# Two loads behind each product for the sample operands, and a step's exponentials written behind the split of the step before

## The chip, the cores and the metric

The kernel runs as one program on one core of a Trainium2 chip. The core has five engines that run side by side and wait for each other through semaphores: TensorE (PE, matrix products, with PEld for its weight loads), VectorE (DVE), ScalarE (ACT), GpSimd (POOL) and SyncE (SP, which here only issues transfers). The metric is the device time of one execution in microseconds (us), lower is better, as the median of several runs.

## The reference

One layer of a decoder is computed for a prompt of 1024 positions and for 8 samples of 8 positions each (64 more columns), with width 1024, all in fp32:

```python
def layer(x, ...):
    h = rmsnorm(x, norm_mix)
    q, k, v, gu, gv, ga, gb = split_in(h @ w_in)
    o  = sink_attention over a window of 128 keys      # 16 heads, 4 kv heads, blocks of 128 queries
    vn = layernorm(gelu(gv));  s = gelu(gu) * (tril(W_s) @ vn + b)   # 128-position chunks, 6 groups
    merged = sigmoid(ga) * (o @ w_branch_attn) + sigmoid(gb) * (s @ w_branch_gmlp)
    x = x + merged @ w_out
    x = x + conv_ffn(rmsnorm(x, norm_ffn))             # up, depthwise conv of width 3, gelu gate, down

def sink_attention(q, k, v, mask, sinks):
    s = where(mask, q @ k.T / 8, -1e30);  m = max(s.max(-1), sink)
    p = exp(s - m);  return (p / (p.sum(-1) + exp(sink - m))) @ v
```

The samples attend to 128 cached keys and values and to their own 8. The last keys and values, the convolution's state and the normalised v rows are outputs too. Both groups end in a final RMSNorm.

## The kernel before

**Operands.** An fp32 product is made of three fp32r products: each operand is split into a high part (a cast on ACT, line 40) and a low part (a subtraction on DVE, line 41), and PE multiplies high by high, high by low and low by high. `split(hi, lo, src)` is this pair. The large products are done by a scheme with seven products of half size (`Chain.product`, line 297).

**Weights.** The class `Weights` keeps the stream of weight tiles: `load` issues the transfers into `wraw` on SP (line 147), `emit` splits a tile into `wh` and `wl`, `get` returns the next one and runs ahead by a given number.

**The columns** are two groups: group 0 has the 64 sample columns and 512 prompt columns, group 1 the other 512.

**The stage of the projections** goes through a list `seq` of column tiles, with seven products each, and calls `behind(at, j)` after each product j. `behind` takes one finished job from `done` (`a_finish`: an activation on ACT, and a store of a gate tile `z` to `sg0d` or `sg1d` on SP, line 874), and then one of three kinds of side work: `jobs`, `lns`, or, when these are used up, `prep`. For the last two entries of `seq`, `prep` holds what `prepare_samples` returns, twelve jobs that only issue transfers and some copies: the queries, keys and masks of the samples, `load_s(0, ...)` for the six operands `s` of group 0 of the gating branch (line 881, 576 KB each), and the caches `ckt` and `cvc` of the samples (line 912). They go out one behind each product with j from 1 to 6.

**The attention stage** runs `attention(gr, pieces)` once for each group. `pieces` are parts of other products (line 237, the gating branch under group 0, the first merge under group 1), nine or twelve matmuls each; `fill()` puts some of them between the attention's steps so that PE has work while a softmax is under way. Under group 0 the samples' attention comes first (`sc_s`, `tr_s`, `pv_s`, `out_s`: scores, transposes, product with v, output); its exponentials are at line 1140. Then the prompt's 16 steps (4 kv heads by 4 blocks) go through a software pipeline, one turn of which, for turn i, is written as:

- `tr_p` of step i-2: four transposes on PE into the one `pt` bank (line 1249), the split of `pt` into `ph` on ACT and `pl` on DVE, and a product `c` on POOL;
- `fill()`;
- `sc_p` of step i: eight score matmuls into `sc` (line 1220), a copy to `s` on ACT (line 1228), a masked copy on DVE (1230, or 1233 for the first block), the row maximum `nm` on DVE (1236), four exponentials with row sums on ACT (1239), reciprocal and multiplication on DVE (1241, 1242);
- `fill()`;
- `pv_p` of step i-3: products with v into `po` (1272, 1277, 1280), a copy `ot` on ACT (1283), two additions `of` on DVE (1288), and the split of `of` into `oh` and `ol`.

**The order.** Each engine does its instructions in one fixed order. This order is made when the program is built, by a scheduler that starts from the written order as a priority and takes an instruction that it holds ready. So a change of the written order can move instructions of every engine in the neighbourhood. Each transfer uses one of eight semaphores in turn, and waits on SP until the transfer eight before it has landed; SP issues in order, so a store that waits for its data holds back the loads behind it.

Of the kernel before, what the change touches and what calls it, by code (L numbers as in the profile page):

```python
# [34 lines left out]
def layer(tc, a):  # L35
# [11 lines left out]
    with ExitStack() as top:  # L47
# [307 lines left out]
        with ExitStack() as ph1:  # L355
# [609 lines left out]
            done, prep, qko = [], [], ExitStack()  # L965
            late["qk"] = poola("qk", 1, qko)

            def behind(at, j):

                if done:  # L970
                    done.pop(0)()
                if jobs:
                    jobs.pop(0)()
                elif lns and at > 5 and j in (0, 2, 4, 6):
                    lns.pop(0)()
                elif prep and j:
                    prep.pop(0)()

            for at, (pair, gs, whole) in enumerate(seq):
                if at == 6:  # L980
# [19 lines left out]
                if gs[0] == 0:  # L1000
# [5 lines left out]
                    prep = prepare_samples()  # L1006
# [88 lines left out]
            def attention(gr, pieces):  # L1095
# [8 lines left out]
                def fill():  # L1104
                    slots["at"] += 1
                    if prep:
                        prep.pop(0)()
                    left = slots["of"] - slots["at"]
                    want = slots["at"] * slots["n"] // (slots["of"] + 4) if left >= 5 else (
                        slots["n"] - (slots["n"] - slots["done"]) * left // (left + 1))  # L1110
                    while slots["done"] < want:
                        pieces[slots["done"]]()
                        slots["done"] += 1
# [3 lines left out]
                if has_s:  # L1117
                    st = {}
# [84 lines left out]
                with tc.tile_pool(name=f"at{g}", bufs=1) as ap:  # L1203
                    gap(ap, (256, 128)[g])
                    steps = [(kv, i) for kv in range(NKV) for i in range(nblk)]
                    st = {}

                    def sc_p(kv, i):
                        if i == 0 and not has_s:
                            oh[kv], ol[kv] = (act.tile([P, 2, n], F32R, name=f"o{x}{kv}") for x in "hl")  # L1210
                        b = gr["blk0"] + i
                        cur = P * i + (P if g else 0)
                        k0 = cur - P if b else cur
                        o0 = 0 if b else P
                        ps = psm.tile([P, 1024], F32, name="sc")
                        ps = ps.rearrange("p (h j) -> p h j", h=4)
                        for h in range(4):
                            q = qt[2 * kv + h // 2][:, h % 2, soff + P * i:soff + P * i + P]
                            for e in range(2):
                                PE.matmul(ps[:, h, o0:256], q, kst[kv][:, e, k0:cur + P],  # L1220
                                          start=e == 0, stop=e == 1)
                        if i == 0:
                            gr["operands"](kv + 1)()
                        if i == 3:
                            gr["values"](kv + 1)()
                        s = ap.tile([P, 4, 132], F32, name="s", bufs=3)[:, :, 0:P + 1]
                        G.tensor_copy(s[:, :, P], late["sinkb"][:, 4 * kv:4 * kv + 4])
                        S.copy(s[:, :, 0:P], ps[:, :, P:256])
                        if b:
                            V.copy_predicated(s[:, :, 0:P], late["mprev"].to_broadcast([P, 4, P]),  # L1230
                                              ps[:, :, 0:P])
                        else:
                            V.copy_predicated(s[:, :, 0:P], late["mprev"].to_broadcast([P, 4, P]),
                                              late["neg"][:, :, None].to_broadcast([P, 4, P]))
                        nm = ap.tile([P, 4], F32, name="nm", bufs=3)
                        V.tensor_reduce(nm, s, AX.X, ALU.max, negate=True)
                        dn = ap.tile([P, 4], F32, name="dn", bufs=3)
                        for h in range(4):
                            S.activation(s[:, h], s[:, h], AF.Exp, bias=nm[:, h:h + 1],  # L1239
                                         accum_out=dn[:, h:h + 1])  # L1240
                        V.reciprocal(dn, dn)
                        V.tensor_mul(s[:, :, 0:P], s[:, :, 0:P], dn[:, :, None].to_broadcast([P, 4, P]))  # L1242
                        st[kv, i] = s

                    def tr_p(kv, i):
                        s = st.pop((kv, i))
                        pt = pst.tile([P, 512], F32, name="pt")
                        for h in range(4):
                            PE.transpose(pt[:, h * P:h * P + P], s[:, h, 0:P], ident)  # L1249
                        ph = ap.tile([P, 512], F32R, name="ph", bufs=2)  # L1250
                        pl = ap.tile([P, 512], F32R, name="pl", bufs=2)
                        split(ph, pl, pt)
                        parts = []
                        if gr["blk0"] + i:
                            c = ap.tile([P, 512], F32R, name="c", bufs=2)
                            cs, fs, ls = (x.rearrange("p (h e q) -> p h e q", h=4, e=2) for x in (c, ph, pl))
                            for src, swap in ((fs, 0), (ls, 1)):
                                for e in range(2):
                                    r, w = 64 * e, 64 * (e ^ swap)
                                    G.affine_select(cs[w:w + 64, :, e], src[r:r + 64, :, e].bitcast(F32),  # L1260
                                                    [[0, 4], [1 - 2 * e, 64]], ALU.is_ge, 0.0, base=-e,
                                                    channel_multiplier=2 * e - 1)
                            parts = [cs]
                        st[kv, i] = [ph, pl, *parts]

                    def pv_p(kv, i):
                        ph, pl, *c = st.pop((kv, i))
                        po = pst.tile([P, 512], F32, name="po")
                        v, d, b = gr["vst"][kv], gr["dvst"][kv], gr["blk0"] + i - gr["b0"]
                        if not c:  # L1270
                            for e, x in enumerate((ph, pl)):
                                PE.matmul(po, v[:, 0], x, start=e == 0, stop=e == 1)
                        else:
                            half = lambda x, e: x.rearrange("p (h e q) -> p h e q", h=4, e=2)[:, :, e]
                            for e in range(2):
                                for x in (ph, pl):
                                    PE.matmul(half(po, e), v[:, b - 1 + e], half(x, e),  # L1277
                                              start=e == 0 and x is ph, stop=False, skip_group_check=True)
                            for e in range(2):
                                PE.matmul(half(po, e), d[:, e, b - 1], c[0][:, :, e], start=False, stop=True,  # L1280
                                          skip_group_check=True)
                        t = ap.tile([64, 512], F32, name="ot")
                        S.copy(t, po[64:128])
                        of = ap.tile([P, 2, P], F32, name="of", bufs=2)
                        tv = t.rearrange("p (a r q) -> p a r q", a=2, r=2)
                        pv = po[0:64].rearrange("p (a r q) -> p a r q", a=2, r=2)
                        for par in range(2):
                            V.tensor_add(of[64 * par:64 * par + 64], pv[:, :, par], tv[:, :, par])
                        c0 = soff + P * i
                        split(oh[kv][:, :, c0:c0 + P], ol[kv][:, :, c0:c0 + P], of)  # L1290

                    for i in range(len(steps) + 3):
                        if i == len(steps):
                            os_.append([(oh[kv][:, e], ol[kv][:, e]) for kv in range(NKV) for e in range(2)])
                        if 2 <= i < len(steps) + 2:
                            tr_p(*steps[i - 2])
                        fill()
                        if i < len(steps):
                            sc_p(*steps[i])
                        if i < len(steps) + 2:  # L1300
                            fill()
                        if i >= 3:
                            pv_p(*steps[i - 3])
# [657 lines left out]
```

## Time and profile before

| | |
|---|---|
| median of 3 runs | 1519.22 us (1518.84 to 1520.51) |
| the profiled execution, its own time | 1514.99 us |
| its span, first to last instruction | 1513.2 us |
| granted TensorE clock, mean | 0.998 |
| PE busy | 1495.6 us (99%), 12202 matmuls |
| PEld busy | 1482.6 us (98%) |
| DVE busy | 1154.9 us (76%) |
| ACT busy | 823.4 us (54%) |
| POOL busy | 268.0 us (18%) |

The prompt's projections end at about 459 us, the samples' attention runs from there to about 492 us, the attention steps of group 0 to about 580 us and those of group 1 from 591 to 678 us. A busy PE is not PE at its peak: matmuls overlap, and a matmul's row lasts longer than the time after which the next can start. So PE's idle time is better read than its share of busy time.

### The profile page before, as it was taken

The numbers are of one execution on the slowest core, as the hardware profiler recorded it, in microseconds if no ns is written. First come the engines' busy times: TensorE is split into PE (matmuls) and PEld (weight loads), VectorE is DVE, ScalarE is ACT, GpSimd is POOL, SyncE is SP. The second block draws the span as 40 slices with busy tenths as digits, with TensorE's granted clock in tenths as the row PEclk, the third lists the DMA queues.
The fourth block names the chain that finished last, engine by engine and source line by source line (L and its number), as shares of the span: only waits on it lengthen the run. The fifth ranks groups of instructions, "written<-read, shape, count | busy, mean of one in ns | idle before, by whom it ended". The sixth has DMA issues, their size and how long they took to land.

```text
span 1513.2 us, 31418 instructions
## 1 busy us (share of the span) xinstructions
PE 1495.6 (99%) x12202; PEld 1482.6 (98%) x12202; DVE 1154.9 (76%) x1915; ACT 823.4 (54%) x1745; POOL 268.0 (18%) x427
## 2 busy tenths in 40 slices
PE   9999999999999999999999999999999999999997
PEld 9999999999998999999999999999999999999997
DVE  5896778756544995989668888898898888785685
ACT  6655764554543774875444555555555556453462
POOL 0000012200020331330222321332142122000003
PEclk9999999999999999999999999999999999999999
DMA  8563557747649758749988323332242226973454
GB/s 282 163 187 112 178 181 256 231 150 274 214 157 326 251 193 230 230 173 301 346 272 282 129 107 123 109 128 108 92 140 109 89 76 225 368 249 97 118 186 133
DMA packets 137508, 286.70 MB, mean 189 GB/s; under 512 B 15248, under 2 KB 44368, under 8 KB 137360
## 3 DMA queue, kind: packets, MB, share of 16 engines
q1 hardware_dynamic: 133040, 280.62, 55.4%
q10 hardware_dynamic: 4320, 4.08, 0.8%
q8 instruction: 96, 1.57, 0.4%
q14 instruction: 52, 0.43, 0.1%
HBM read 195.76 MB, written 90.85 MB: 189 GB/s over the span
## 4 chain that ended last, share of the span: by engine, by line
PE 66%; DVE 5%; DMA 5%; issue 3%; ACT 3%; POOL 1%; SPq 1%; POOLq 0%; DVEq 0%; ACTq 0%
PE st L297 40%; PE mm L237 12%; PE dn L1721 10%; DMA wraw<-wt 2%; DVE wl L41 1%; PE sc L1220 1%; DMA q<-qd 1%; DMA vst<-vd 1%; POOL x L1786 1%; ACT s L1239 1%; PE mx L834 1%; PE pt L1249 1%; DMA wraw<-wpb 0%; DVE s L1242 0%; PE po L1277 0%
## 5 line engine op out<-in xcount | busy, mean ns | idle before, releaser
L297 PE MATMUL st<-th,wh 128*128 128x256 f32 (+1 forms) x2128 | 610.9, 287 | 1.9 <-ACT kn L280 0.7
L297 PE MATMUL st<-tl,wh 128*128 128x256 f32 (+1 forms) x2128 | 608.8, 286 | 0.0
L297 PE MATMUL st<-th,wl 128*128 128x256 f32 (+1 forms) x2128 | 608.4, 286 | 0.0
L297 PEld LDWEIGHTS st<-th,wh 128*128 128x128 f32 x2128 | 400.1, 188 | 3.7 <-ACT k L278 1.6
L297 PEld LDWEIGHTS st<-th,wl 128*128 128x128 f32 x2128 | 400.4, 188 | 0.0
L297 PEld LDWEIGHTS st<-tl,wh 128*128 128x128 f32 x2128 | 399.9, 188 | 0.0
L40 ACT CAST wh<-wraw 128x512 fp32r<-128x512 f32 (+2 forms) x204 | 139.5, 694 | 99.4 <-PE st L297 36.4
L41 DVE TENSOR_TENSOR wl<-wraw,wh 128x512 fp32r<-128x512 f32 (+2 forms) x204 | 159.9, 796 | 39.5 <-ACT wh L40 37.3
L1721 PE MATMUL dn<-th,wh 128*128 128x288 f32 (+1 forms) x616 | 176.8, 287 | 0.0
L1721 PE MATMUL dn<-tl,wh 128*128 128x288 f32 (+1 forms) x616 | 176.3, 286 | 0.0
L1721 PE MATMUL dn<-th,wl 128*128 128x288 f32 (+1 forms) x616 | 175.1, 284 | 0.0
L40 ACT CAST wh<-ws 128x512 fp32r<-128x512 f32 x160 | 98.1, 622 | 97.0 <-PE st L297 61.6
L41 DVE TENSOR_TENSOR wl<-ws,wh 128x512 fp32r<-128x512 f32 x160 | 109.3, 695 | 50.4 <-ACT wh L40 48.7
L1721 PEld LDWEIGHTS dn<-th,wl 128*128 128x128 f32 x616 | 115.9, 188 | 0.0
L1721 PEld LDWEIGHTS dn<-tl,wh 128*128 128x128 f32 x616 | 115.7, 188 | 0.0
L1721 PEld LDWEIGHTS dn<-th,wh 128*128 128x128 f32 x616 | 115.6, 188 | 0.0
L285 POOL TENSOR_TENSOR z<-kn,k 128x256 f32<-128x256 f32 (+1 forms) x32 | 28.2, 883 | 315.9 <-ACT kn L280 300.3
L40 ACT CAST th<-traw 128x544 fp32r<-128x544 f32 (+1 forms) x85 | 53.9, 642 | 46.6 <-PE dn L1721 32.0
L237 PE MATMUL mm<-s,wh 128*128 128x256 f32 (+1 forms) x384 | 77.2, 294 | 1.2 <-DMA s<-sd 1.2
L41 DVE TENSOR_TENSOR tl<-traw,th 128x544 fp32r<-128x544 f32 (+1 forms) x85 | 61.2, 728 | 20.2 <-ACT th L40 20.0
L528 PE MATMUL st<-w2h,th 128*128 128x256 f32 x308 | 74.2, 282 | 0.5 <-DVE th L45 0.2
L237 PE MATMUL mm<-ol,wh 128*128 128x256 f32 (+1 forms) x256 | 73.7, 289 | 0.3 <-DVE ol L41 0.3
(294 smaller groups left out, 3153.1 us busy)
## 6 DMA issues: line engine op xcount, KB each, us to landing
wraw<-wt SPq DMA_DIRECT2D x133, 512.0 KB
traw<-td SPq DMA_DIRECT2D x77, 272.0 KB
td<-za SPq DMA_DIRECT2D x22, 544.0 KB
wraw<-wt SPq DMA_DIRECT2D x35, 256.0 KB
upd<-hl SPq DMA_DIRECT2D x14, 512.0 KB
td<-t SPq DMA_DIRECT2D x11, 544.0 KB
qd<-q SPq DMA_DIRECT2D x8, 576.0 KB
q<-qd SPq DMA_DIRECT2D x8, 576.0 KB
```

The source lines that it names most:

```text
L40: S.copy(hi, src)
L41: V.tensor_sub(lo, src, hi.bitcast(F32))
L237: PE.matmul(ps[:, lo:lo + c1 - c0], u[:, k, :], v[:, c0:c1], start=(clear and k == 0 and i == 0), stop=(k == nk - 1 and i == 2), skip_grou ...
L285: op(to, pick(x, to, lo, hi), pick(y, to, lo, hi))
L297: PE.matmul(ps, u[:, kk, :], v, start=first and kk + i == 0, stop=kk == 3 and i == 2, skip_group_check=True)
L528: PE.matmul(ps, u, v[:, k, :], start=k + i == 0, stop=k == KD - 1 and i == 2)
L834: PE.matmul(ps[:, P * i:P * i + P], vn[:, i], late["wst"][:, c, :], start=True, stop=True)
L1220: PE.matmul(ps[:, h, o0:256], q, kst[kv][:, e, k0:cur + P], start=e == 0, stop=e == 1)
L1239: S.activation(s[:, h], s[:, h], AF.Exp, bias=nm[:, h:h + 1], accum_out=dn[:, h:h + 1])
L1249: PE.transpose(pt[:, h * P:h * P + P], s[:, h, 0:P], ident)
L1721: PE.matmul(place(m, e), u[:, m, :], v[:, lo:hi], start=new and i + k == 0 and (e == 0 or m % 2 == 0), stop=i == NU - 1 and k == 2, skip_g ...
L1786: G.tensor_mul(xc, xc, rs)
```

## The change

In `behind`, two jobs of `prep` are issued behind each product instead of one. The twelve jobs are then issued behind the six products that used to take the first six.

In the prompt's attention, `sc_p` ends with the row maximum. What followed it (exponentials, reciprocal, multiplication) becomes a function `soft`, and turn i calls `soft` of step i-1 behind `tr_p` of step i-2 and ahead of the first `fill()`. The instructions themselves stay the same in number and shape.

```diff
@@ behind
                 elif prep and j:
-                    prep.pop(0)()
+                    for go in prep[:2]:
+                        go()
+                    del prep[:2]
@@ sc_p
                         nm = ap.tile([P, 4], F32, name="nm", bufs=3)
                         V.tensor_reduce(nm, s, AX.X, ALU.max, negate=True)
+                        st[kv, i] = s, nm
+
+                    def soft(kv, i):
+                        s, nm = st[kv, i]
                         dn = ap.tile([P, 4], F32, name="dn", bufs=3)
                         for h in range(4):
                             S.activation(s[:, h], s[:, h], AF.Exp, bias=nm[:, h:h + 1],
@@ the turns
                         if 2 <= i < len(steps) + 2:
                             tr_p(*steps[i - 2])
+                        if 1 <= i <= len(steps):
+                            soft(*steps[i - 1])
                         fill()
```

In the rows below, the line numbers of the changed kernel are larger by 2 behind `behind` and by 6 behind `soft`. Rows are in the order of the engine; `s` with a number behind it is one of the six branch operands, `sd` its copy in memory, and `x2` means two equal instructions.

SP, at the end of the projections, where the sample loads stand. Before:

```order
L881 DMA s_6000<-sd_164 128x1152
L874 DMA sg0d_138<-z_5691 128x512
L874 DMA sg1d_146<-z_5692 128x512
L881 DMA s_6038<-sd_165 128x1152
L912 DMA cvc<-cv 128x512
L881 DMA s_6073<-sd_166 128x1152
L147 DMA wraw<-wpb 128x768 x2
L881 DMA s_6098<-sd_167 128x1152
L912 DMA ckt<-ckt 128x1088
L912 DMA cvc<-cv 128x512
```

Now:

```order
L881 DMA s_5946<-sd_164 128x1152
L881 DMA s_5967<-sd_165 128x1152
L912 DMA cvc<-cv 128x512
L881 DMA s_5991<-sd_166 128x1152
L881 DMA s_5993<-sd_167 128x1152
L912 DMA ckt<-ckt 128x1088
L912 DMA cvc<-cv 128x512
L874 DMA sg0d_138<-z_5691 128x512
L874 DMA sg1d_146<-z_5692 128x512
L147 DMA wraw<-wpb 128x768 x2
```

Six loads have moved ahead of the two gate stores, and three of them (the last operand `s`, `ckt` and the last `cvc`) also ahead of the two weight loads `wraw<-wpb` that they stood behind.

ACT, in the steps of group 0, around the eighth and ninth `ot` copy. Before:

```order
L40 CAST oh_6493<-of 128x2x128
L1228 COPY s<-sc 128x4x128
L1283 COPY ot<-po 64x512
L1239 ACTIVATE s,dn<-s,nm 128x129 x4
L40 CAST oh_6493<-of 128x2x128
L40 CAST ph<-pt 128x512
L1228 COPY s<-sc 128x4x128
L1283 COPY ot<-po 64x512
L40 CAST ph<-pt 128x512
```

Now:

```order
L40 CAST oh_6493<-of 128x2x128
L1245 ACTIVATE s,dn<-s,nm 128x129 x2
L1230 COPY s<-sc 128x4x128
L1289 COPY ot<-po 64x512
L40 CAST ph<-pt 128x512
L1245 ACTIVATE s,dn<-s,nm 128x129 x2
L40 CAST oh_6493<-of 128x2x128
L1245 ACTIVATE s,dn<-s,nm 128x129 x2
L1230 COPY s<-sc 128x4x128
```

The cast `ph` stood behind a set of four exponentials and the `oh` cast at this place, and now stands ahead of them; the `oh` cast, which stood behind all four, stands between the second and the third.

PE, in the steps of group 0, around the fourth set of transposes. Before:

```order
L1280 MATMUL po<-c,dvst 128x4x64 x2
L237 MATMUL mm<-s_6162,wh 128x256 x2
L237 MATMUL mm<-s_6162,wl 128x256
L237 MATMUL mm<-s_6164,wh 128x256 x2
L1249 MATMUL pt<-c_ident,s 128x128 x4
L237 MATMUL mm<-s_6164,wl 128x256
L237 MATMUL mm<-s_6166,wh 128x256 x2
L237 MATMUL mm<-s_6166,wl 128x256
L1220 MATMUL sc<-kst,q 128x256 x8
```

Now:

```order
L1286 MATMUL po<-c,dvst 128x4x64 x2
L1255 MATMUL pt<-c_ident,s 128x128 x4
L237 MATMUL mm<-s_6162,wh 128x256 x2
L237 MATMUL mm<-s_6162,wl 128x256
L237 MATMUL mm<-s_6164,wh 128x256 x2
L237 MATMUL mm<-s_6164,wl 128x256
L237 MATMUL mm<-s_6166,wh 128x256 x2
L237 MATMUL mm<-s_6166,wl 128x256
L1222 MATMUL sc<-kst,q 128x256 x8
```

Five matmuls of a branch piece stood ahead of the transposes and now stand behind them; the scores stay where they were.

## The prediction

> **What bounds the kernel now.** I read the busy shares first, then busy time by stretch, then what PE waited for, and last the timelines of the waits found. The page gives:
>
> ```profile
> span 1513.2 us, 31418 instructions
> ...
> PE 1495.6 (99%) x12202; PEld 1482.6 (98%) x12202; DVE 1154.9 (76%) x1915; ACT 823.4 (54%) x1745; POOL 268.0 (18%) x427
> ```
>
> The busy times by stretch (length; then PE, PEld, DVE, ACT, POOL; clock, DMA share, GB/s) show where PE's missing 17.6 us can be touched by this change:
>
> ```profile
> 500.00:565.00 65.00, 62.73 (x501) 60.52 (x500) 60.24 (x116) 49.91 (x159) 22.07 (x52) 1.00 0.67 214
> ...
> 593.00:678.00 85.00, 83.10 (x648) 80.28 (x648) 74.73 (x141) 63.63 (x198) 30.83 (x77) 1.00 0.71 220
> 678.00:770.00 92.00, 91.95 (x745) 91.75 (x744) 66.39 (x88) 40.14 (x55) 12.47 (x9) 1.00 0.92 316
> 770.00:1420.00 650.00, 649.58 (x5291) 648.28 (x5290) 534.85 (x815) 339.58 (x653) 134.61 (x188) 1.00 0.45 154
> ```
>
> From 678 to 1420 us PE idles 0.5 us in 742. So what is won or lost ahead of 678 us goes through to the end, since what follows is paced by PE. In the attention steps PE idles 2.27 us in the first stretch and 1.90 in the second, and DVE is nearly as full there (60.24 of 65). The waits of PE from 440 to 680 us (total, times, longest):
>
> ```profile
> PE pt L1249 <- DVE s L1242: 1.8, 4, 0.8
> PE mm L237 <- DMA s<-sd: 1.2, 1, 1.2
> PE pt L1249 <- DVE pl L41: 0.9, 1, 0.9
> PE po L1277 <- DVE of L1288: 0.5, 1, 0.5
> PE sc L1220 <- DMA q<-qd: 0.3, 1, 0.3
> PE mm L237 <- DVE ol L41: 0.3, 1, 0.3
> ```
>
> The whole change is about the first three rows, 3.9 us: the transposes wait for the softmax of their step (1.8) or for their bank to be read (0.9), and one product waits for a sample operand (1.2).
>
> A recorded gap is shorter than the true one. Of the chain of waits one row gives the pace of the matmuls, 2.08 / 18 = 0.116 us each; of the groups of lines one gives their length, 278 ns (x is the count, then busy, mean, idle):
>
> ```profile
> 536.47 2.08 PE mm L237 x18
> ```
>
> ```profile
> L1249 PE MATMUL pt<-c_ident,s 128*128 128x128 f32 x128 | 19.9, 278 | 3.1 <-DVE s L1242 1.8 <-DVE pl L41 0.9
> ```
>
> The gap is counted from the end of the last matmul, while the next could have started 0.28 - 0.116 = 0.16 us before that. Each wait is worth its row plus 0.16.
>
> **Edit 1, two loads behind each product.** SP's timeline, and the same time by stretch:
>
> ```profile
> 445.25 0.45 SPq L881 DMA_DIRECT2D s<-sd  x1
> 451.07 0.32 SPq L874 DMA_DIRECT2D sg0d<-z  x1
> ...
> 454.21 0.91 SPq L147 DMA_DIRECT2D wraw<-wpb  x2
> 455.16 0.49 SPq L881 DMA_DIRECT2D s<-sd  x1
> ```
>
> ```profile
> 445.70:451.10 5.40, 5.40 (x50) 5.40 (x49) 4.18 (x7) 2.45 (x6) 3.09 (x7) 1.00 1.02 384
> 451.10:454.20 3.10, 3.10 (x29) 3.10 (x28) 1.22 (x2) 2.62 (x6) 0.00 (x0) 1.00 0.85 279
> 454.20:460.50 6.30, 6.30 (x66) 5.96 (x66) 2.23 (x4) 2.61 (x5) 0.74 (x1) 1.00 0.97 355
> 460.50:465.00 4.50, 3.35 (x34) 2.82 (x33) 2.65 (x4) 3.47 (x5) 0.00 (x0) 1.00 1.03 404
> ```
>
> SP issues nothing from 445.70 to 451.07, since the store of `z` waits for its data and the loads stand behind it. The engines run on what is queued until 451.1, then drop to 279 and 355 GB/s. Against the best stretch, 404, that is room for (404 - 279) x 3.1 + (404 - 355) x 6.3 = 0.70 MB, or 1.7 us at 404. The six loads now come ahead of the stores, and their bytes can fill this room. No instruction is added; the stores themselves are issued a few us later and nobody reads them soon.
>
> The Trainium skill, "Perfetto Trace Analysis", section "Roofline", states that a core that is active alone is bounded by its 16 DMA engines, at about 435 GB/s together. The trace stays below, with 404 at most. By that figure the room would be about 1.3 MB (an estimate, 51 x 5.4 + 156 x 3.1 + 80 x 6.3), the transfers 2.9 us earlier instead of 1.7, the first term below -0.8, and the sum 1515.7.
>
> What PE and ACT did with these transfers (PE's timeline, the chain of waits):
>
> ```profile
> 463.90 0.56 PE L237 MATMUL mm<-s,wh 128*128 128x320 f32 x2 [1.15 <-DMA s<-sd]
> ...
> 467.31 0.27 PE L1153 MATMUL pt<-c_ident,s 128*128 128x128 f32 x1
> ```
>
> ```profile
> 454.21 7.15 DMA wraw<-wpb
> ...
> 463.15 0.83 ACT wh L40
> ...
> 464.00 1.28 ACT L1140
> ...
> 465.29 0.90 ACT s L1140 x4
> ...
> 466.22 0.29 DVE sx L1143
> ```
>
> The last operand `s`, issued at 455.16 and awaited until 463.90, now goes ahead of the stores and of both `wpb` loads (768 x 128 x 4 = 0.39 MB each, 1.9 us at 404 together). It gains 1.7 and 1.9 us, so the wait of 1.15 + 0.16 = 1.3 us is gone. The price stands behind it. The `wpb` loads now follow `s`, `ckt` and the last `cvc` of that group, 0.59 + 0.56 + 0.26 = 1.41 MB, 3.5 us; less 1.7 they land up to 1.8 us later. ACT casts them (`wh`) ahead of the sample exponentials, in its fixed order. The first landed at 454.21 + 7.15 = 461.36 and the second cast began at 463.15, so between none and all of the 1.8 is slack. The sample sums end at 466.22 + 0.29 = 466.51, PE comes to their transposes at 467.31; without its wait it comes at 466.0. If ACT is late by d, PE waits 0.5 + d there, and the edit is worth 1.3 - 0.5 - d. I take d = 0.2, small, since the slack of the first cast is nearest: **-0.6**, from -1.3 (PE finds other work to be first) to +1.0 (d = 1.8).
>
> The product of the last samples' values is moved too:
>
> ```profile
> 483.12 0.33 SPq L912 DMA_DIRECT2D cvc<-cv  x1
> ...
> 489.61 0.43 PE L1170 MATMUL po<-cvc,pts 128*32 128x64 f32 x16
> ```
>
> It stood 6.5 us behind the issue of its cache load; PE's new order has it some 18 matmuls (2.08 us) earlier. That is 4.4 us after that issue if the load stays put: 0, at worst +2.1.
>
> **Edit 2, the exponentials behind the split.** The transposes of three turns of group 0, and ACT and DVE between them, and the group of the reciprocals from 500 to 565 us:
>
> ```profile
> 539.11 0.60 PE L1249 MATMUL pt<-c_ident,s 128*128 128x128 f32 x4
> ...
> 544.21 0.66 PE L1249 MATMUL pt<-c_ident,s 128*128 128x128 f32 x4 [0.86 <-DVE pl L41]
> ...
> 549.89 0.63 PE L1249 MATMUL pt<-c_ident,s 128*128 128x128 f32 x4 [0.81 <-DVE s L1242]
> ```
>
> ```profile
> 540.63 0.41 ACT L1239 ACTIVATE s<-s,nm 128x129 f32<-128x129 f32 x1 [0.69 <-DVE nm L1236]
> ...
> 542.19 0.39 ACT L40 CAST oh<-of 128x256 fp32r<-128x256 f32 x1
> 542.61 0.59 ACT L40 CAST ph<-pt 128x512 fp32r<-128x512 f32 x1
> ```
>
> ```profile
> 542.32 0.18 DVE L1241 RECIPROCAL dn<-dn 128x4 f32<-128x4 f32 x1 [0.97 <-ACT s L1239]
> 542.53 0.69 DVE L1242 TENSOR_TENSOR s<-s,dn 128x512 f32<-128x512 f32 x1
> ```
>
> ```profile
> L1241 DVE RECIPROCAL dn<-dn 128x4 f32<-128x4 f32 x13 | 2.3, 175 | 3.6 <-ACT s L1239 3.6
> ```
>
> The transposes of 539.11 were done at 539.71, but ACT stood idle 0.69 us up to 540.63 and then did four exponentials and `oh` before `ph` at 542.61. The one bank `pt` was free only after `pl`, so the next transposes waited to 544.21, and the turn behind was late as well (0.81). This is the place that the order rows of ACT show: `ph` now stands ahead. It fits into the idle 0.69 us (it lasts 0.59), so it costs the exponentials nothing. Both waits go: 0.86 + 0.81 + 2 x 0.16 = **-2.0** (from 0 to -2.0). In the other turns the scheduler had `ph` ahead of the exponentials already, so there is nothing of this kind to win.
>
> The other three waits for `s` of L1242 are 1.8 - 0.81 = 1.0, with 3 x 0.16 1.5 us. The cast of `oh` now lies inside the exponentials, which holds the sums back by 0.39, but they start earlier where `ph` is. I take two thirds: **-1.0** (0 to -1.5).
>
> Against this: in about 8 of the 16 turns of group 0 PE's order had some five matmuls of a branch piece between `po` and the transposes, and now has none (the order rows of PE). They are still done, but no longer cover the end of the softmax. Where the softmax ends first nothing is lost. Where it doesn't, at most 5 x 0.116 = 0.58 us is lost a turn. I take one half of one turn, **+0.3**, since the waiting row above names only four turns of 32 in which PE came before the multiplication; the ends are 0 (an order cannot gain from less cover) and 8 x 0.58 = +4.6.
>
> **The sum.** -0.6 - 2.0 - 1.0 + 0.3 = -3.3 us. The profiled execution took 1514.99 us for its span of 1513.2, so 1511.7 there. The median of the runs shown lies 4.23 us above it; the same difference gives **1515.9 us**.
>
> **Rivals.**
>
> *Transfers at their limit, and half of the turns.* The engines are at 1.02 from 445.7 to 451.1 already and at 1.03 while PE waits. If the 0.70 MB of room isn't there for these loads, the wait changes its place from the operand to the sample transposes (d = 0.8 gives 1.3 - 0.5 - 0.8 = 0). If of edit 2 only half comes, since ACT's order had already what the change says save at that place, -1.5, and the new waits are +0.5: -1.0, **1518.2**. For it: the shares, and the order. Against it: 279 GB/s in the middle.
>
> *The transposes lose their cover (slower).* Place: the transposes of group 0, behind `po`. Mechanism: the multiplication L1242 ends after PE's last `po` matmul, and the five matmuls that filled the gap stand behind it. It decides from the point where that multiplication ends later than the last L1280 matmul; then each such turn pays up to 0.58. With 8 turns +4.6, nothing of the 3.0 above, and edit 1 at -0.6: +4.0, **1523.2**. For it: the multiplication of 542.53 ended at 543.22, and PE had nothing of `po` left then; DVE is 93% busy, so it can't catch up; waits for that line are already the largest row. Against it: the exponentials start no later than before where `ph` fits a hole of ACT, and DVE waits 3.6 us for them in all, time it would win back.
>
> *All of it.* The 3.6 us that DVE idles before the reciprocals shrink as well, and with them the waits on `of` and `ol` (0.5, 0.3): -1.3 - 2.0 - 1.5 - 0.8 - 2 x 0.16 - 0.6 for smaller gaps, -6.5, **1512.7**. Against it: DVE would need to be under 93%.
>
> **How the numbers follow.** The forecast 0.50 (by the ends of its terms from -4.8 to -1.8: 1514.4 to 1517.4), transfers at their limit 0.22, lost cover 0.20, all of it 0.08. A measurement of this kernel can tell about 0.2%, 3.0 us, from no change: 1516.2 and 1522.3. Of the forecast's own cases some three fifths lie beyond 1516.2, with the last rival 0.30 + 0.08, rounded up to 0.40 faster. Same is the rest and the first rival, 0.40; slower the second, 0.20. The range runs from below the best case, 1512.0, to 1522.0, which leaves out most of the slower rival.
>
> **What would show it.** Right: no wait of `mm` for `s<-sd` near 463 us; `ph` within 1 us of the transposes' end in every turn; no row `pt <- DVE pl`; `pt <- DVE s` under 1 us. Wrong: PE waiting at L1155 for the samples' `s`, or `wh` of `wpb` starting a microsecond later (edit 1 given back); `pt L1255 <- DVE s L1248` at 3 us or more in eight or so short waits (lost cover); PE idle between 500 and 565 us above 2.27.

## The result: slower by 0.17%, and the profile after

The changed kernel took 1522.5 us (median of 21 runs, 1517.75 to 1526.03) against 1520.51 us for the kernel before in the same runs (21 runs). The ratio is 1.0017, with a 95% interval of 1.0009 to 1.0024, which is +2.6 us (1.4 to 3.6). The forecast was -3.3 us. In the last group of runs three executions, two of the kernel before and one of the changed kernel, took 2101.70 to 2467.18 us at a granted clock of 0.555 to 0.653, and they are in no ratio.

The stretches of the profile after (length; PE, PEld, DVE, ACT, POOL; clock, DMA share, GB/s):

```profile
460.00:465.00 5.00, 3.98 (x39) 3.51 (x40) 1.86 (x5) 3.09 (x6) 0.74 (x1) 1.00 0.67 197
465.00:485.00 20.00, 19.31 (x209) 17.09 (x208) 11.97 (x35) 7.71 (x26) 0.19 (x1) 1.00 1.00 339
485.00:500.00 15.00, 14.17 (x123) 13.39 (x123) 10.11 (x25) 7.89 (x25) 0.63 (x4) 1.00 0.96 297
500.00:565.00 65.00, 62.96 (x505) 60.89 (x505) 60.34 (x115) 49.22 (x158) 21.02 (x52) 1.00 0.66 211
593.00:678.00 85.00, 82.87 (x639) 79.20 (x638) 74.88 (x139) 63.50 (x198) 32.46 (x77) 1.00 0.72 220
1300.00:1450.00 150.00, 150.00 (x1204) 150.00 (x1204) 106.68 (x191) 69.61 (x125) 0.00 (x0) 1.00 0.59 195
```

The same stretches of before, where the prediction did not show them:

```profile
460.00:465.00 5.00, 3.85 (x46) 3.10 (x38) 2.65 (x4) 3.82 (x6) 0.00 (x0) 1.00 1.03 407
465.00:485.00 20.00, 20.00 (x222) 17.98 (x215) 10.64 (x34) 6.70 (x26) 0.42 (x2) 1.00 0.99 316
485.00:500.00 15.00, 14.90 (x126) 14.06 (x127) 9.18 (x23) 6.74 (x25) 0.62 (x4) 1.00 0.97 298
1300.00:1450.00 150.00, 150.00 (x1224) 150.00 (x1223) 109.50 (x196) 70.93 (x128) 0.00 (x0) 1.00 0.60 199
```

PE's idle time of after, stretch by stretch, against before: 1.02 and 0.69 against 1.15 and 0 up to 485 us (+0.56), 0.83 against 0.10 up to 500 (+0.73), 2.04 against 2.27 in the steps of group 0 (-0.23), 2.13 against 1.90 in those of group 1 (+0.23). That is +1.29 us recorded. PE's waits from 440 to 700 us in the changed kernel:

```profile
PE pt L1255 <- DVE s L1248: 3.4, 9, 0.8
PE sc L1130 <- ACT s L1135: 1.0, 1, 1.0
PE sc L1222 <- DMA q<-qd: 0.5, 1, 0.5
PE mm L237 <- DVE ol L41: 0.4, 1, 0.4
PE pt L1156 <- DVE sx L1145: 0.4, 1, 0.4
PE pt L1155 <- ACT s L1142: 0.3, 1, 0.3
PE pt L1255 <- ACT wh L40: 0.2, 1, 0.2
```

These are 15 waits where before listed nine. With 0.16 us for each of the six more, 1.29 + 0.96 = 2.25 us, an estimate close to the measured time. Two of the rows aimed at are gone: no `mm <- s<-sd`, no `pt <- pl`. In their place PE waits three times in the samples' attention and nine times instead of four for the multiplication.

The profiled executions are 5.1 us apart in their spans (1518.3 and 1513.2), more than this. The last row of each table shows where the rest is from: from 1300 to 1450 us, where the code is the same, 1204 matmuls instead of 1224 were done in 150 us, at the same granted clock and with PE busy throughout; 20 x 0.1225 us is 2.5 us. A second profile of the changed kernel doesn't show it (below), and the profiles of seven other runs, some of them without either edit, do; so it belongs to the execution and not to the change.

**What held the samples.** SP, ACT and PE of the changed kernel, from their timelines:

```profile
446.48 0.97 SPq L881 DMA_DIRECT2D s<-sd  x2
...
450.71 0.33 SPq L874 DMA_DIRECT2D sg0d<-z  x1
452.15 0.33 SPq L874 DMA_DIRECT2D sg1d<-z  x1
```

```profile
456.67 0.38 ACT L280 ACTIVATE kn<-st 128x256 f32<-128x256 f32 x1 [0.64 <-PE st L297]
461.51 0.39 ACT L315 ACTIVATE z<-st 128x256 f32<-128x256 f32 x1 [4.46 <-DMA sg1d<-z]
...
463.37 0.39 ACT L1135 COPY s<-sc 128x272 f32<-128x272 f32 x1 [0.40 <-ACT z L872]
463.65 1.57 ACT L40 CAST wh<-wraw 128x768 fp32r<-128x768 f32 x2
```

```profile
463.81 0.67 PE L1130 MATMUL sc<-ckt,qs 64*32 64x136 f32 x16 [1.02 <-ACT s L1135]
...
467.09 0.33 PE L1155 MATMUL pt<-c_ident,s 128*128 128x128 f32 x1 [0.30 <-ACT s L1142]
467.81 0.30 PE L1156 MATMUL pt<-c_ident,sx 128*64 128x128 f32 x1 [0.39 <-DVE sx L1145]
```

The store `sg1d<-z` was issued at 452.15, 0.23 us earlier than before (452.38). But its data now stood behind six more loads in the transfer engines, and it released its buffer only at 461.51, 9.36 us after its issue. The next projection tile writes into the same buffer `z`, so ACT stood still for 4.46 us, and behind it, in its fixed order, the copy of the sample scores, the casts `wh` and the sample exponentials. PE waited 1.02 us for the copy and 0.30 + 0.39 at the transposes. In the kernel before the same activation did not wait for any store:

```profile
459.97 0.38 ACT L315 ACTIVATE z<-st 128x256 f32<-128x256 f32 x1 [0.46 <-PE st L297]
```

### The profile page after: what moved, and what is told of

The parts are those of the page before. It is cut to its first block, busy times and chain, and to the rows that moved or that the text cites. A ratio compares the mean times of both kernels' runs of the same rounds, so it can differ in the third digit from the quotient of the medians.

```text
span 1518.3 us, 31425 instructions
## 1 busy us (share of the span) xinstructions
PE 1499.4 (99%) x12202; PEld 1485.8 (98%) x12202; DVE 1158.0 (76%) x1915; ACT 822.9 (54%) x1745; POOL 270.9 (18%) x427
## 4 chain that ended last, share of the span: by engine, by line
PE 69%; DVE 4%; DMA 3%; ACT 3%; issue 3%; POOL 1%; SPq 1%; POOLq 0%; ACTq 0%; DVEq 0%
PE st L297 39%; PE mm L237 13%; PE dn L1729 12%; PE sc L1222 1%; ACT s L1245 1%; PE pt L1255 1%; POOL x L1794 1%; DVE wl L41 1%; PE mx L834 1%; PE po L1283 1%; DMA sg1d<-z 1%; DMA q<-qd 1%; DMA wraw<-wt 0%; DMA s<-sd 0%; ACT wh L40 0%
```

## The experiments

All ratios are against the kernel before, run on the same chip at the same time. Per cent of 1520 us: 0.1% is 1.5 us.

### Edit 1 alone

```diff
-                    prep.pop(0)()
+                    for go in prep[:2]:
+                        go()
+                    del prep[:2]
```

> Edit 1 alone. Theory (a store that is issued at the same time lands some 5 us later, because the loads issued ahead of it fill the transfer engines; its buffer z stays taken, and ACT, in its fixed order, stands behind that): ACT's activation L315 into z waits 4 to 5 us for the store sg1d<-z, PE's second sample scores wait about 1 us for ACT's copy, the sample transposes 0.5 to 1 us more, and the wait of 1.15 us for the last operand s is gone: +0.5 to +1.5 us, all of it ahead of 475 us. Rival (edit 1 gains and edit 2 alone loses): PE idles less than before ahead of 475 us, -0.6 us.

Measured: 1518.91 us, ratio 1.0013 (1.0003 to 1.0024), +2.0 us. ACT's and PE's waits:

```profile
ACT z L315 <- DMA sg1d<-z: 4.5, 1, 4.5
```

```profile
PE pt L1251 <- DVE s L1244: 3.3, 9, 0.7
PE sc L1130 <- ACT s L1135: 1.1, 1, 1.1
PE pt L1251 <- ACT s L1230: 0.9, 1, 0.9
...
PE pt L1156 <- DVE sx L1145: 0.4, 1, 0.4
PE pt L1155 <- ACT s L1142: 0.3, 1, 0.3
```

The waits at the store and in the samples came as expected; the time lies above the expected range, and that the loss lies all ahead of 475 us did not hold. The first row is the surprise: nine waits of the prompt's transposes, as in the whole change, in a kernel whose attention code is that of before. What differs is the order. The scheduler ordered the steps of group 0 anew: in eleven turns one after the other PE had the transposes directly behind `po`, where before had four to ten matmuls of a piece between them in six of these. The sixth set of transposes of group 0 with edit 1, and the tenth of the kernel before, which stood directly behind `po` already and did not wait:

```profile
518.03 0.39 PE L1282 MATMUL po<-c,dvst 128*128 128x256 f32 x2
518.67 0.63 PE L1251 MATMUL pt<-c_ident,s 128*128 128x128 f32 x4 [0.25 <-DVE s L1244]
```

```profile
538.87 0.40 PE L1280 MATMUL po<-c,dvst 128*128 128x256 f32 x2
539.11 0.60 PE L1249 MATMUL pt<-c_ident,s 128*128 128x128 f32 x4
```

Not all of the nine waits stand in such turns: two (0.67 and 0.18 us) are those of the first two sets of transposes, which have nine matmuls ahead of them, one (0.63) stands behind two matmuls, and two (0.6 us) are in group 1.

### Edit 2 alone

The diff of `sc_p`, `soft` and the turns, without that of `behind`.

> Edit 2 alone. Theory (lost cover): the wait for the last operand s is back at 1.15 us as before; the transposes wait for the multiplication in 8 to 10 turns, 3 to 4 us recorded in all, and not for pl: PE idles in the steps some 1 to 1.5 us more than before, +1 to +1.5 us. Rival (the loss of the whole change is that of the loads, and the steps gain): the waits of the transposes are under 2 us in all, -1 to -3 us.

Measured: 1518.29 us, ratio 1.0009 (0.9998 to 1.002), +1.4 us, in the expected range, but not clear of zero. Its profile can't be used for the stage of the samples: in that execution the last operand came late, and PE's granted clock fell to 0.83, as the mean of the stretch behind it (0.50 from 465.5 to 472 us).

```profile
PE mm L237 <- DMA s<-sd: 3.0, 1, 3.0
PE pt L1253 <- DVE s L1246: 1.7, 5, 0.8
PE pt L1253 <- ACT ot L1287: 0.8, 1, 0.8
```

```profile
465.00:485.00 20.00, 19.46 (x186) 17.28 (x187) 9.69 (x28) 7.59 (x25) 0.43 (x2) 0.83 0.97 316
```

The second row is a miss: 1.7 us in five waits, not 3 to 4 in eight to ten; that the time agreed is luck. The row for `pl` is gone, but a wait of 0.8 us for `ot` has come. So the nine waits of the whole change come with edit 1's order.

### Edit 1 with buffers of its own for the last z

```diff
+                if at == len(seq) - 1:
+                    zpa = poola("zb", 1)
                 zs = {g: [zpa.tile(...
```

> Edit 1, and the last projection tile writes z into buffers of its own, so that no activation has to wait for a store. Theory of the taken buffer: ACT's wait of 4 to 5 us for sg1d<-z is gone, and with it PE's wait at the second sample scores; the sample exponentials then start when the second weight tile wpb has landed and is cast, at about 465.3 us as before, so that some 0.5 to 1 us of wait remains at the sample transposes: -0.3 us against before (-0.8 to +0.2). Rival (the late wpb loads hold ACT, not the store): PE waits as in the run of edit 1 alone, +0.5 to +1.5 us.

Measured: 1516.25 us, ratio 0.9995 (0.9982 to 1.0007), -0.8 us, at the edge of the expected range and not clear of zero. ACT at the activation that waited, and PE's waits:

```profile
459.10 0.39 ACT L315 ACTIVATE z<-st 128x256 f32<-128x256 f32 x1 [0.40 <-PE st L297]
```

```profile
PE pt L1253 <- DVE s L1246: 1.8, 4, 0.8
PE pt L1253 <- DVE pl L41: 0.8, 1, 0.8
PE mm L237 <- DMA s<-sd: 0.5, 1, 0.5
```

The waits for the store and for ACT's copy are gone with the buffer, so it was the taken buffer that held ACT. The late `wpb` loads didn't: the scheduler put their casts behind the first sample exponentials. No wait is listed at the sample transposes, where 0.5 to 1 us was expected. PE's order in group 0 was that of before again, and with it the four and one waits; so it is not the order of the loads alone that ordered the steps anew, but the loads with the shared buffer. A part of the wait for `s` has moved to a later product (0.5). Between edit 1 alone and this kernel lie 2.7 us by the ratios, for the stall and the order together; the times do not separate the two, the traces do (below).

### Control: the buffers without the loads

The same two lines in the kernel before.

> Control: the kernel before with the z buffers of its own and nothing else. Before, the store sg1d<-z that was issued at 452.38 did not hold ACT, so these buffers take nothing away: 0 (within 0.7 us), with PE's wait for the last operand s still 1 us or so. If the gain of the run of edit 1 with these buffers came from the buffers and not from the loads: -0.8 us or more.

Measured: 1519.58 us, ratio 1.0 (0.9989 to 1.0011). As expected, the buffers alone give nothing.

### The whole change with these buffers

> The whole change with z buffers of its own for the last tile. PE's order of the samples is that of before again, and the steps are those of edit 2 alone. If the two edits add up: the loads with the buffers -0.9, edit 2 alone +1.2, in all about +0.3 us against before (-0.5 to +1.0). If edit 2 only loses in the order that edit 1 brings about: -0.9 or less.

Measured: 1520.12 us, ratio 1.0007 (0.9992 to 1.0022), +1.1 us, just above the range expected from adding up, and with an interval that takes in both cases: inconclusive by itself. It says no more than that edit 2, on top of mended loads, brought no gain. In its profile a later product waited 1.8 us for an operand `s`, where the kernel without edit 2 had 0.5.

### Edit 2, and the kernel before, with a piece of work ahead of the transposes

Two kernels; in the first with `soft` behind `tr_p`, in the second without edit 2.

```diff
+                        fill()
                         if 2 <= i < len(steps) + 2:
                             tr_p(*steps[i - 2])
-                        fill()
```

> Edit 2 with the first fill() of a turn written ahead of the transposes instead of behind the exponentials: in group 0 nine matmuls of a piece stand again between po and the transposes. Theory (lost cover): the waits of the transposes for the multiplication in group 0, about 3 us in the run of the whole change, go to under 0.5 us; against before -1.5 to -3 us. Rival (the softmax itself ends too late, behind the split on ACT or for want of DVE, whatever PE does meanwhile): the waits stay near 3 us, or show at po instead, and the time is that of edit 2 alone.

> The kernel before with only the first fill() of a turn written ahead of the transposes, so that nine matmuls of a piece stand between po and the transposes in nearly every turn of group 0. Lost cover: the transposes' waits for the multiplication in group 0 (some 2.4 us recorded for s and pl before) go to under 1 us, -1.5 us or more. DVE's pace (it is busy 60 of 65 us, and whatever PE does meanwhile the multiplications come no faster): waits stay at 2 to 3 us, within 0.7 us of before.

Measured: with edit 2 1517.56 us, ratio 1.0001 (0.9991 to 1.0011); without 1516.07 us, ratio 0.9979 (0.9967 to 0.9992), -3.2 us, the fastest of all by its ratio. The transposes' waits, first of edit 2's kernel, then of the other:

```profile
PE pt L1253 <- DVE s L1246: 1.9, 5, 0.8
PE pt L1253 <- ACT ot L1287: 0.7, 1, 0.7
```

```profile
PE pt L1249 <- DVE s L1242: 0.9, 3, 0.5
...
PE pt L1249 <- DVE pl L41: 0.7, 1, 0.7
```

In both, nine matmuls stood between `po` and the transposes in most turns of group 0. With the steps written as before the time fell as the lost-cover theory had it, and the expectation for DVE's pace missed. The profile shows only a part of it: PE's listed waits fell from 5.0 to 4.0 us in all, and behind the steps PE was 0.79 us ahead of before. With edit 2 the waits stayed (1.9 us in five), as the rival had it, for which the softmax itself ends late; the expectation of a gain of 1.5 to 3 us missed.

### Is it DVE's pace? The subtraction for ol on GpSimd

In `pv_p`, once in the whole change, once in the kernel with edit 1 and the buffers:

```diff
-                        split(oh[...], ol[...], of)
+                        hi, lo = oh[...], ol[...]
+                        S.copy(hi, of)
+                        G.tensor_sub(lo, of, hi.bitcast(F32))
```

> The whole change, with the subtraction that makes ol moved from DVE to GpSimd (0.46 us of DVE a turn); PE's order in group 0 stays that of the whole change, with the transposes directly behind po. DVE's pace: DVE's busy time from 500 to 565 us falls from 60.3 to about 55 us, the transposes' waits for the multiplication fall from 3.4 us to under 1.5, -1.5 to -3 us against the whole change, so about 0 or somewhat faster against before. Lost cover alone (the chain ACT exponentials, multiplication, transposes is too long for the turn): the waits stay near 3 us and the time within 0.7 us of the whole change, +2 us against before.

> Edit 1 with the z buffers of its own, the steps written as before, and the subtraction for ol on GpSimd: a candidate that beats both. The z buffers alone were worth -0.8 to -1.0 us against before. DVE's pace: another -1.5 to -2.5, in all -2.3 to -3.5 us. If DVE isn't what the transposes wait for: -1 us as with the z buffers alone, or slower by GpSimd's longer subtraction where po pieces wait for its masks c.

Measured: 1521.95 us, ratio 1.0019 (1.0007 to 1.0031), and 1517.88 us, ratio 0.9993 (0.9981 to 1.0006). Of the first:

```profile
500.00:565.00 65.00, 61.64 (x493) 59.16 (x493) 57.65 (x102) 48.83 (x155) 31.25 (x61) 1.00 0.65 212
```

```profile
PE pt L1255 <- DVE s L1248: 3.6, 8, 0.8
```

DVE was relieved by 2.7 us in the stretch, less than expected, and the waits did not fall; both times are those without this edit. So relieving DVE did not shorten the waits. The second kernel is no clean test, since its order changed as well: from the sixth set on, eleven turns of group 0 had no matmul between `po` and the transposes, and yet the transposes waited for the multiplication hardly longer than before (1.9 us in five against 1.8 in four).

### Is it ACT's order? The cast for oh on GpSimd

`G.tensor_copy(hi, of)` in place of `S.copy`, in the whole change, in the kernel before, and in edit 1 with buffers and `fill()` first.

> The whole change, with the cast that makes oh moved from ACT to GpSimd; the transposes stand directly behind po as in the whole change. Theory of the loop (transposes, split ph, exponentials with oh in their middle, reciprocal, multiplication, next transposes: 4.66 us from 544.55 to 549.21 in the changed kernel, against about 4.2 us of PE work in a turn with 18 matmuls): without oh, which takes 0.30 us between two exponentials, the loop is 4.3 to 4.4 us, the recorded waits of the transposes for the multiplication in group 0 (eight of 0.17 to 0.7 us) lose some 0.2 to 0.3 us each, 3.4 us in all go to under 2, and the time is 1 to 2 us below that of the whole change, +0.5 to +1.5 against before. If oh doesn't count, the waits stay at 3 us or more and the time at +2 to +2.6 us.

> The kernel before with the cast for oh on GpSimd instead of ACT, without either edit. In the whole change the same step brought the time from +2.6 to -1.5 us against before. If that was because edit 2 puts oh between the exponentials, then here, where oh stood behind all four, it brings little: 0 to -1.5 us. If the cast is worth 4 us wherever it stood (ACT's load), -3 to -4 us.

> Candidate: edit 1, z buffers of its own, fill() ahead of the transposes, the cast for oh on GpSimd. In ACT's order the exponentials then stand ahead of the split ph in most turns of group 0, so that the transposes of a step don't hold the exponentials of the next. Waits of the transposes in group 0 under 1 us, -2.5 to -5 us against before. If the turns are not bound by ACT at this point: as the same without the cast, -1.7.

Measured: 1518.04 us, ratio 0.999 (0.9982 to 0.9999); 1515.76 us, ratio 0.9986 (0.9972 to 0.9999); 1516.39 us, ratio 0.9989 (0.9974 to 1.0003). The loop that the first expectation speaks of is this turn of the changed kernel (PE, ACT, DVE):

```profile
544.55 0.63 PE L1255 MATMUL pt<-c_ident,s 128*128 128x128 f32 x4 [0.28 <-DVE s L1248]
...
549.21 0.63 PE L1255 MATMUL pt<-c_ident,s 128*128 128x128 f32 x4 [0.28 <-DVE s L1248]
```

```profile
545.22 0.59 ACT L40 CAST ph<-pt 128x512 fp32r<-128x512 f32 x1 [0.27 <-PE pt L1255]
...
547.05 0.39 ACT L40 CAST oh<-of 128x256 fp32r<-128x256 f32 x1
...
547.35 0.40 ACT L1245 ACTIVATE s<-s,nm 128x129 f32<-128x129 f32 x1
```

```profile
548.17 0.17 DVE L1247 RECIPROCAL dn<-dn 128x4 f32<-128x4 f32 x1
548.37 0.69 DVE L1248 TENSOR_TENSOR s<-s,dn 128x512 f32<-128x512 f32 x1
```

Without the cast on ACT the whole change went from +2.6 (+2.1 in its repeat) to -1.5 us, more than expected, but the waits did not do what the loop theory said:

```profile
PE pt L1255 <- DVE s L1248: 3.6, 9, 0.7
```

The kernel before gained 2.1 us by the same step, where `oh` stood behind all four exponentials. So some half of the gain has nothing to do with edit 2. What is left, about 1.5 to 2 us, could be the place between the exponentials, but the intervals overlap. The loop theory isn't shown. By the count below, the whole change with this cast was 1.4 us faster behind the steps than without, and 1.0 of it came between the 1000th and the 1200th matmul, at the first steps of group 1, where the wait for `q` (0.5) was no longer listed; not in the turns of group 0 of which the theory speaks. The third kernel came out at -1.7 us, as without the cast, and the expectation of -2.5 to -5 missed.

### The loads mended and the fill first

> The kernel before with edit 1, z buffers of its own for the last tile, and the first fill() of a turn ahead of the transposes: a version that should beat both. The two parts alone measured -0.8 and -3.2 us by their ratios; if they add up, -3 to -4.5 us against before. If the gain of either is a matter of luck in the order of the scheduler that the other upsets, -1 us or less.

Measured: 1517.26 us, ratio 0.9989 (0.9978 to 1.0), -1.7 us. Faster than before by its estimate, with an interval that just reaches it, but the two parts (-0.8 and -3.2) did not add up.

### The whole change once more

> The whole change once more, unchanged, on the chip and at the time of the two others, so that they are compared with it under the same conditions: +1 to +3.5 us against before (its first ratio was 1.0017, 1.0009 to 1.0024).

Measured: 1519.05 us (eleven executions), ratio 1.0014 (1.0001 to 1.0026), +2.1 us. In its profile ACT waited 4.3 us for the store, the transposes 3.5 us in nine waits. From 1300 to 1450 us it did 1222 matmuls, nearly as before.

### The same matmuls, counted

By the prediction's own arithmetic a delay of under 0.16 us leaves no gap, so the lists of waits can miss some. A count does not. Up to the last matmul of the projections PE's order is the same in the kernels below, and 250, 410, 600, 1000, 1200 and 1770 matmuls later each has done the same number of each kind and shape. In the kernel before these six start 23.45, 43.17, 67.34, 118.97, 145.60 and 220.35 us behind that last one (at 483, 503, 527, 578, 605 and 680 us). The table gives how much later they start in the other kernels, each from the timeline of its one profile:

| | 250th | 410th | 600th | 1000th | 1200th | 1770th |
|---|---|---|---|---|---|---|
| whole change | +0.83 | +1.12 | +1.80 | +0.81 | +1.02 | +1.84 |
| whole change, once more | +0.59 | +1.23 | +1.88 | +0.89 | +1.08 | +1.86 |
| edit 1 alone | +0.89 | +1.25 | +1.99 | +1.87 | +2.09 | +2.17 |
| edit 1 with buffers | -0.68 | -0.68 | -0.67 | -0.87 | -1.52 | -1.43 |
| whole change with buffers | +0.66 | +0.65 | +0.71 | +1.09 | +1.59 | +2.42 |
| buffers alone (control) | +0.21 | +0.19 | +0.23 | +0.03 | +0.34 | +0.43 |

The control, with PE's order of before, says how far such a difference can be off: by up to 0.4 us. The samples stand ahead of the 250th: there the stall costs 0.6 to 0.9 us, and the buffers take it away. From there to the 600th the three kernels with the new order of group 0 lose another 1.0 to 1.3 us, and the others nothing. From the 600th to the 1000th, where the wait for `pl` stood, the whole change wins back 1.0 us, and edit 1 alone 0.1; without the new order of group 0 (fifth row) edit 2 loses 0.4 there. From the 1200th to the 1770th, in the steps of group 1, every kernel with edit 2 and its casts on ACT loses 0.73 to 0.83 us (five profiles), and those without edit 2 lose 0.05 to 0.09 (five). The waits listed in these steps do not show it: 1.7 us before and 1.7 now. What it is made of stays open.

## Why the prediction was wrong

**Edit 1, the stores.** The step that failed first is the clause that the stores are issued later and nobody reads them soon. They were issued no later. But whether someone reads them was the wrong question: the next tile writes their buffer, and a store behind a full queue releases it late. The repeat and the run of edit 1 alone show the same stall (4.3 and 4.5 us), the separate buffers remove it. The Trainium skill, "Perfetto Trace Analysis", section "Identifying Performance Opportunities" (Optimization Strategy), says that a gap that repeats on the engine that should be saturated can mean that there was no memory for the next tile. Here the gap is single and on ACT, and one more set of buffers removed it. The term was put at -0.6 with ends from -1.3 to +1.0; PE's idle time up to 485 us grew by 0.56 recorded, and with two more waits by 0.9 in all, within the ends but by another mechanism. What the prediction said on the other side held: the wait of 1.15 us for `s` went, and part of it came back at the sample transposes (0.30 + 0.39), though because of the store and not of the `wpb` loads. It was not won for good either: in the five kernels with the early loads and the buffers a later product waited 0.5 to 1.8 us for its operand `s`, against 0.5 to 1.3 us, and once 3.0, in the six with the loads of before.

**The last cvc.** That value product, moved 18 matmuls earlier, did not matter in itself: the repeat lists 0.2 us for it. What mattered and was not thought of: the early loads, with the shared buffer, came with a new order of the samples' end and of the steps of group 0. How the one leads to the other is not shown.

**Edit 2, the two waits.** That the wait for `pl` would go was right: the row is gone. The value of 2.0 us was not kept: by the count the whole change won 1.0 us at this place, and with the buffers edit 2 won nothing there. The other waits for the multiplication, which were to fall by 1.0 us, grew from 1.8 us in four to 3.4 in nine.

**The lost cover.** This term was mis-sized, and put to the wrong edit. It was taken at half of one turn, +0.3; the new order of group 0, which edit 1 alone brings about, cost 1.0 to 1.3 us up to the 600th matmul. That the missing cover is the reason is shown only in part. In the kernel before, the two waits for the multiplication in group 0 (0.33 and 0.81 us) stood in turns that had five matmuls of cover, and the six turns without any had no such wait. In the changed kernel five of the nine (1.6 us) stand in turns without cover, but two (0.8 us) are those of the first two sets of transposes, with nine matmuls ahead. The run with `fill()` ahead (-3.2 us) speaks for cover, the eleven turns without it in the kernel with `ol` on GpSimd against it, though DVE was relieved there as well. So the rival on the slower side named this place, at a chance of 0.20, and its 1523.2 us came near the measured 1522.5 by luck: it counted edit 1 as a gain and eight turns at the full 0.58 us, and the kernel before itself came out 1.3 us above the 1519.22 us from which it started.

**Group 1.** The prediction had no term for the steps of group 1, though `soft` is called there too. There the kernel lost 0.7 to 0.8 us, in each of the five profiles with edit 2 and its casts on ACT.

**The ends.** The stretch from -4.8 to -1.8 us is not what the ends of the terms give: those on the slow side add up to +5.6 us, so that its own terms took in a loss that the range left out.

**Where it went, in all.** By the count of the first profile the whole change lost 0.83 us in the samples and 0.97 in the first turns of group 0, won 0.99 in the later ones, and lost 0.21 between the groups and 0.82 in the steps of group 1: 1.84 us, where +2.6 (1.4 to 3.6) and +2.1 were measured. Of edit 1's share the stall is thus somewhat less than half. Edit 2 was forecast as the larger gain; in the kernels that differ in it alone the time with it was longer each time, by 0.1 to 0.6 us on top of edit 1, 1.4 alone, 1.9 with the buffers and 3.3 with `fill()` first, of which only the last comes near to being clear of noise. Why its steps of group 1 last longer stays open, and so does what `fill()` first gained beyond the waits.

## What to carry to other kernels

When loads are moved ahead of a store, ask not only when the store is issued and who reads it, but when its data leave, and who waits to write the buffer again: here a release that had come within 7.6 us (452.38 to 459.97, where ACT met no wait for it) took 9.4 us with six loads ahead of it. Where a scheduler makes the order, cost a change by the order of the whole program and not only at the lines that it touches: a few lines on loads gave the steps of a later stage another order. A wait that shows in few turns is no measure of what the other turns do in another order. And a list of waits is not the whole loss: compare the times at which two kernels have done the same work, stage by stage.

## What the runs showed of the hardware

A store of 256 KB released its buffer 9.36 us after its issue where loads were queued ahead of it. The same matmuls, with PE busy throughout and the granted clock at 1.00, were paced 1.6% slower in one execution (1204 against 1224 in 150 us) and not in another of the same kernel (1222); of the profiles of the other runs seven show the slower count (1197 to 1206), five the faster (1222 or 1224), and one lies between (1211). After PE had stood idle for 3.0 us, one execution showed a granted clock of 0.50 from 465.5 to 472 us; waits of 1.15 and 1.82 us were not followed by this. In the same execution the transfer engines moved 411 to 427 GB/s from 462.5 to 472 us, more than the 404 that the prediction took as the most.
